# Eight feed-forward tiles that take x1·A2 and nine shift columns, with the second root applied to their sums

## Chip, cores and metric

One core of a Trainium2 chip runs the program. The metric is the device time of one execution in microseconds (us), a median over runs. A profiled execution also has a span, from its first to its last instruction.

## The reference

One layer of a decoder on 320 columns: 256 prompt positions and 8 sequences of 8 sample positions, 2048 features. The part that matters here is where the first sub-layer ends and the feed-forward begins. `m` is the output projection of the mixed heads, `gt1`, `sc2` and `sh2` come from a modulation vector per sequence (one for the prompt, one for each sample).

```python
m = concat(ret_out, sgu_out) @ w_o
x = x + gt1 * rmsnorm(m, g_post_mix)                 # x1
h2 = rmsnorm(x, g_pre_ffn) * (1 + sc2) + sh2
f = square(relu(h2 @ w_ff1)) @ w_ff2                 # 8192 inner features
x = x + gt2 * rmsnorm(f, g_post_ffn)
```

Every matrix product is made in float32 from three products of a reduced form: each operand is split into a high and a low part, and high·high, low·high and high·low are added up.

## The kernel before

Features stand on the 128 partitions, in 16 tiles (KB) of 320 columns (T): TP = 256 prompt columns, then TS = 64 sample columns. A weight piece is one load of 1 MB issued by SP (`load_w`): ScalarE (ACT) casts each half of it into `wh`, VectorE (DVE) subtracts to get `wl`, and a tile of output costs 16 times `mm3`, three TensorE (PE) products each with a weight load. Two raw buffers (NRAW) and three pairs of halves (NHALF) rotate.

Four banks (`acc`) hold running sums. `project` runs a matrix output tile by output tile, one bank each; only the first four tiles of w_o and of w_ff1 are made together, input tile by input tile, in all four banks, from pieces stored for that purpose. `done` evicts a tile: in the feed-forward it is `done_1`, a Relu on ACT out of the bank, a square on GpSimd (POOL) and a `split` into high (ACT) and low (DVE).

Between w_o and the feed-forward lies the residual chain. `mean_rsqrt(sums["m"])` gives the first root `rm`. For each of the 16 tiles DVE makes `gm = gm*rm` and `x1 = x1 + gm`, ACT squares x1, and `mean_four` sums the squares of four tiles on PE in four groups of 32 rows. From these sums comes the second root `r2`: DVE copies them out, PE adds the groups (`thirty`), ACT and DVE take the root. Then `modulate` makes `h2 = x1*A2*r2 + SH2`, split in two, for each tile; A2 and SH2 hold nine columns per tile, the prompt's and eight of the samples. The first product of w_ff1 needs the h2 of tile 0. While the chain runs, PE makes the eight prompt states (`prompt_state`, four instructions each) and products of constants that nobody reads (`keep_warm`, L132).

Modulation columns are made a few at a time from w_ada: four loads of 1 MB (`steps`), 32 PE instructions (`ada_products`), then `ada_finish`: a DVE transpose, four PE products with `sel` and DVE scaling. Two such groups for A2 and SH2 are made around the chain (`late`), further ones (`ada_c`, for G2) beside the first tiles of w_ff1.

The code stands in the order of one engine-neutral program. A scheduler puts it in order per engine, by priorities: `ahead()` raises one, `tc.keep_in_program_order` pins an instruction to its place. Every engine then runs its own list in order, and SP its list of loads.

## Time and profile before

| | us |
|---|---|
| median of 3 runs | 1581.99 (1581.36 to 1582.89) |
| the profiled execution, time | 1581.7 |
| the profiled execution, span | 1579.9 |
| PE busy | 1550.3 (98% of the span) |
| DVE, ACT, POOL busy | 803.7, 578.1, 168.9 |
| mean DMA rate | 205 GB/s |

The share of busy time is high on PE in every part, dummy products among it. What a stretch does is read from the windows and the timeline, in us from the start of the span.

### The profile page before, as it was taken

The page shows a single profiled execution, that of the slowest core. Times are in us where ns is not written, and L with a number is a line of the kernel's source. Part 1 is how long each engine was busy: PE and PEld are TensorE (multiplying, and loading weights), DVE is VectorE, ACT ScalarE, POOL GpSimd, SP SyncE. Part 2 cuts the span into 40 slices and gives each one's busy share as a digit, 9 for nine tenths or more (in the row PEclk, how much of TensorE's full clock was granted, in tenths as well). Part 3 has the DMA queues.
Part 4 walks back from the last instruction along what each step waited for, and adds up shares of the span by engine and source line. Part 5 has one row for each costly group of instructions (what it writes and reads, how often), then busy time and mean ns, then how long its engine had stood idle before and what let it go on. Part 6 is the DMA issues. An engine that isn't in the chain of part 4 may idle for free.

```text
span 1579.9 us, 25805 instructions
## 1 busy us (share of the span) xinstructions
PE 1550.3 (98%) x10900; PEld 1447.1 (92%) x10900; DVE 803.7 (51%) x1319; ACT 578.1 (37%) x843; POOL 168.9 (11%) x176
## 2 busy tenths in 40 slices
PE   8999999999999999999999999999999999999995
PEld 6798898888889997789999999999999999999995
DVE  5776566777744446744433344444444444444555
ACT  5332235234433333433333344322344333443331
POOL 0000000001000120421100112000121000221211
PEclk9999999999999999999999999999999999999998
DMA  8978888665777445784444434434344343443442
GB/s 353 379 307 329 309 327 320 243 247 198 274 271 279 170 153 205 281 311 160 157 147 147 160 136 158 152 142 160 139 155 154 140 160 142 152 158 137 159 146 82
DMA packets 57155, 323.91 MB, mean 205 GB/s; under 512 B 5584, under 2 KB 18128, under 8 KB 22096
## 3 DMA queue, kind: packets, MB, share of 16 engines
q1 hardware_dynamic: 56464, 320.98, 54.3%
q8 instruction: 85, 1.39, 0.3%
q10 hardware_dynamic: 576, 1.29, 0.2%
q14 instruction: 30, 0.25, 0.0%
HBM read 314.65 MB, written 7.60 MB: 204 GB/s over the span
## 4 chain that ended last, share of the span: by engine, by line
PE 95%; DVE 2%; DMA 1%; ACT 1%; issue 0%; POOL 0%; SPq 0%; DVEq 0%; ACTq 0%; POOLq 0%
PE acc L295 28%; PE acc L297 28%; PE acc L296 28%; PE ada L202 5%; DVE f L112 1%; PE pn L546 1%; DMA adaw<-in_w_ada_dram 1%; PE pm L173 1%; DMA x<-in_x_dram 1%; PE acc L132 0%; DVE wl L112 0%; DVE z L112 0%; PE adaT L222 0%; PE gate L440 0%; PE po L524 0%
## 5 line engine op out<-in xcount | busy, mean ns | idle before, releaser
L295 PE MATMUL acc<-hi,wh 128*128 128x320 f32 x3072 | 953.4, 311 | 2.9 <-ACT wh L285 1.5
L296 PE MATMUL acc<-lo,wh 128*128 128x320 f32 x3072 | 951.5, 310 | 0.3 <-DVE lo L112 0.2
L297 PE MATMUL acc<-hi,wl 128*128 128x320 f32 x3072 | 950.0, 310 | 1.1 <-DVE wl L112 1.0
L112 DVE TENSOR_TENSOR wl<-raw,wh 128x1024 fp32r<-128x1024 f32 (+1 forms) x386 | 470.4, 1220 | 485.7 <-ACT wh L285 468.6
L285 ACT CAST wh<-raw 128x1024 fp32r<-128x1024 f32 (+1 forms) x386 | 402.8, 1044 | 744.8 <-PE acc L296 699.6
L295 PEld LDWEIGHTS acc<-hi,wh 128*128 128x128 f32 x3072 | 576.3, 188 | 13.4 <-issue 7.0
L296 PEld LDWEIGHTS acc<-lo,wh 128*128 128x128 f32 x3072 | 576.7, 188 | 7.9 <-issue 6.4
L297 PEld LDWEIGHTS acc<-hi,wl 128*128 128x128 f32 x3072 | 576.2, 188 | 7.3 <-issue 5.0
L112 POOL TENSOR_TENSOR a<-rl 128x320 f32<-128x320 f32 x64 | 87.8, 1371 | 705.2 <-ACT rl L815 682.5
L202 PE MATMUL ada<-adaw,csil 128*32 128x512 f32 (+1 forms) x800 | 88.0, 578 | 0.3 <-DMA adaw<-in_w_ada_dram 0.3
L112 DVE TENSOR_TENSOR z<-z,acc 128x320 f32<-128x320 f32 x120 | 57.2, 484 | 49.4 <-PE acc L297 48.6
L112 POOL TENSOR_TENSOR sq<-sq,sq 128x320 f32<-128x320 f32 x28 | 39.7, 1419 | 275.8 <-ACT sq L751 275.7
L112 DVE TENSOR_TENSOR lo<-a,hi 128x320 fp32r<-128x320 f32 x64 | 31.5, 493 | 71.3 <-ACT hi L304 71.3
L202 PEld LDWEIGHTS ada<-adaw,csil 128*32 128x32 f32 x800 | 23.4, 109 | 47.5 <-issue 45.6
L304 ACT CAST hi<-a 128x320 fp32r<-128x320 f32 x64 | 29.4, 459 | 96.5 <-POOL a L112 96.5
L112 DVE TENSOR_TENSOR f<-f,acc 128x320 f32<-128x320 f32 x48 | 23.4, 488 | 67.7 <-PE acc L297 67.7
L112 POOL TENSOR_TENSOR ve<-vts,cst 128x256 f32<-128x256 f32 x16 | 14.0, 902 | 179.5 <-DVE vts L496 179.1
L218 DVE STREAM_TRANSPOSE part<-ada 128x512 f32<-128x512 f32 (+1 forms) x25 | 17.3, 691 | 26.8 <-PE ada L202 26.7
L815 ACT ACTIVATE rl<-acc 128x320 f32<-128x320 f32 x64 | 27.5, 430 | 1.2 <-PE acc L297 1.2
L112 POOL TENSOR_TENSOR mt<-mt,A 128x64 f32<-128x64 f32 x20 | 8.7, 436 | 177.4 <-DVE A L232 176.1
L317 ACT ACTIVATE hi<-mt,SH 128x256 fp32r<-128x256 f32 x32 | 16.3, 509 | 25.1 <-DVE mt L311 20.7
L320 DVE SCALAR_TENSOR_TENSOR lo<-mt,SH,hi 128x256 fp32r<-128x256 f32 x32 | 15.8, 493 | 3.3 <-ACT hi L317 3.3
(165 smaller groups left out, 569.9 us busy)
## 6 DMA issues: line engine op xcount, KB each, us to landing
raw<-in_w_ff_dram SPq DMA_DIRECT2D x128, 1024.0 KB, 4.8
adaw<-in_w_ada_dram SPq DMA_DIRECT2D x96, 1024.0 KB, 7.9
raw<-in_w_in_dram SPq DMA_DIRECT2D x33, 1024.0 KB, 6.0
raw<-in_w_o_dram SPq DMA_DIRECT2D x16, 1024.0 KB, 4.8
raw<-in_w_in_dram SPq DMA_DIRECT2D x13, 960.0 KB, 4.9
s<-in_s_dram SPq DMA_DIRECT2D x8, 512.0 KB, 5.7
out_ss_dram<-s SPq DMA_DIRECT2D x8, 512.0 KB, 3.7
x<-in_x_dram SPq DMA_DIRECT2D x4, 640.0 KB, 6.7
```

The lines of the kernel that those rows point to most:

```text
L112: return (eng or V).tensor_tensor(out=out, in0=a, in1=b, op=op)
L173: PE.matmul(pm[32 * j : 32 * j + 32, :T], ones[:, :32], q[j], start=first, stop=last, tile_position=(0, 32 * j))
L202: mm = PE.matmul(acc[32 * j : 32 * j + 32, :ncol], csil[:, kb, :], ws[kb // nk][:, kb % nk * ncol : (kb % nk + 1) * ncol], start=i < 4, st ...
L218: V.transpose(part[:, :ncol], acc[:, :ncol])
L285: S.copy(wh[:, :n], r)
L295: PE.matmul(acc[:, :T], wh, ah, start=start, stop=False)
L296: PE.matmul(acc[:, :T], wh, al, start=False, stop=False)
L297: PE.matmul(acc[:, :T], wl, ah, start=False, stop=stop)
L304: S.copy(hi, src)
L317: S.activation(hi[:, :TP], t[:, :TP], AF.Identity, bias=Sm[:, f, 0:1])
L320: V.scalar_tensor_tensor(out=lo[:, :TP], in0=t[:, :TP], scalar=Sm[:, f, 0:1], in1=hb[:, :TP], op0=ALU.add, op1=ALU.subtract)
L815: S.activation(rl, acc[:, :T], AF.Relu)
```

## The change

Eight of the 64 tiles of w_ff1 no longer take h2. Since r2 is one number per column, and SH2 one vector per sequence, `W·h2 = r2 * (W·(x1*A2)) + W·SH2`. So a tile's input becomes `hs`: x1*A2, 256 + 64 columns, and behind them the nine columns of SH2 and a zero, 330 columns in all (TX), split into `hx` and `lx`.

- Tiles 0 to 3 are made inside the residual chain, two input tiles per pass p. For each pair DVE makes gm and x1 (`residual`), ACT the high part of the prompt columns (`high`), POOL copies the shift columns and DVE makes the sample columns (`samples`), ACT casts them (`high_s`), DVE makes both low parts (`low`) and ACT squares (`square`). Weight halves are prepared in the same passes (`half_w`, its low part last). `mean_four` follows behind the products. `keep_warm` is gone; four prompt states stand ahead of the chain and four in it, the latter in banks of another pool.
- At the end the four sums are copied to slots (`evict_1`), and r2 is made while the next tiles run. `done_1` multiplies a copied sum by r2 (DVE), adds the shift to the sample columns (DVE), and takes the Relu with the prompt's shift as bias (ACT).
- Tiles 4 to 7 are again four together, and still take `hs`. Tiles 8 to 11 are four together on the true h2, which `extra` makes, two input tiles beside each piece of tiles 4 to 7 and four beside the first pieces of tiles 8 to 11.
- Slots grow from 320 to 330 columns, and NSLOT goes from 89 to 87. The host stores the pieces of tiles 4 to 11 in the four-together form.

```diff
--- before.py
+++ after.py
-NSLOT = 89
+NSLOT = 87
...
-    def mean_four(pm, q, first, last):
+    def mean_four(pm, q, first, last, pin=None):
 
         for j in range(4):
-            PE.matmul(pm[32 * j : 32 * j + 32, :T], ones[:, :32], q[j], start=first, stop=last, tile_position=(0, 32 * j))
+            mm = PE.matmul(pm[32 * j : 32 * j + 32, :T], ones[:, :32], q[j], start=first, stop=last, tile_position=(0, 32 * j))
+            if pin and j == 0:
+                pin(mm)
...
+    def ada_drain(feats, acc):
+
+        ncol = P * len(feats)
+        part = wp.tile([P, 512], F32, tag="part", bufs=1, name=nm("part"))
+        V.transpose(part[:, :ncol], acc[:, :ncol])
+        return feats, part
+
     def ada_finish(feats, acc):
+        ada_scale(*ada_sums(*ada_drain(feats, acc)))
+
+    def ada_sums(feats, part):
 
         nf = len(feats)
         ncol = P * nf
-        part = wp.tile([P, 512], F32, tag="part", name=nm("part"))
-        V.transpose(part[:, :ncol], acc[:, :ncol])
         pv = part[:, :ncol].rearrange("p (i q r) -> p i q r", i=nf, q=4)
         pt = small("adaT")
         for q in range(4):
             PE.matmul(pt[32 * q : 32 * q + 32, : 9 * nf], sel, pv[:, :, q, 0:9], start=True, stop=True, tile_position=(0, 32 * q))
+        return feats, pt
+
+    def ada_scale(feats, pt):
...
+    def half_w(w, c0, pin=None, nb=8, behind=None):
+
+        n = P * nb
+        wh = wp.tile([P, 1024], F32R, tag="wh", bufs=NHALF, name=nm("wh"))
+        wl = wp.tile([P, 1024], F32R, tag="wl", bufs=NHALF, name=nm("wl"))
+        r = w[:, P * c0 : P * c0 + n]
+        ins = S.copy(wh[:, :n], r)
+
+        def low_part():
+            ins = tt(wl[:, :n], r, wh[:, :n].bitcast(F32), ALU.subtract)
+            if pin:
+                pin(ins)
+
+        blocks = [(wh[:, i : i + P], wl[:, i : i + P]) for i in range(0, n, P)]
+        if pin:
+            pin(ins)
+            return blocks, low_part
+        with tc.issue_after(behind) if behind is not None else nullcontext():
+            low_part()
...
+        n = ah.shape[1]
+        PE.matmul(acc[:, :n], wh, ah, start=start, stop=False)
+        PE.matmul(acc[:, :n], wh, al, start=False, stop=False)
+        PE.matmul(acc[:, :n], wl, ah, start=False, stop=stop)
...
-    def prompt_state():
+    def prompt_state(bank):
         h, kt, vt = later.pop(0)
-        pp = new_acc()
+        pp = bank()
...
+    TX = T + 10
+    def evict_1(acc):
+        u = slot("u", F32, (P, TX))
+        S.copy(u, acc[:, :TX])
+        return u
...
+    for _ in range(4):
+        prompt_state(new_acc)
...
+    pin = tc.keep_in_program_order
     pm1 = small("pm")
-    for q in range(4):
+    acc_1 = [new_acc() for _ in range(4)]
+    raws = [load_raw(A["w_ff1"][i]) for i in range(2)]
+    w_1 = [half_w(raws[0], 0), half_w(raws[0], 8), half_w(raws[1], 0)]
+    hs = [None] * KB
+    t4 = [None] * 4
+    dve = [None]
+
+    def residual(fs):
+        for f in fs:
+            pin(tt(gm[f], gm[f], rm, ALU.mult))
+        for f in fs:
+            pin(tt(x1[f], x1[f], gm[f], ALU.add))
+
+    def samples(f, n):
+
+        q, j = f // 4, f % 4
+        if t4[q] is None:
+            t4[q] = slot("ts")[:, : 4 * (TX - TP)].rearrange("p (i c) -> p i c", i=4)
+            G.memset(t4[q][:, :, TS:], 0.0)
+        G.tensor_copy(t4[q][:, j : j + n, TS : TS + 9], SH2[:, f : f + n, :])
+        pin(tt(t4[q][:, j : j + n, :TS].rearrange("p i (b s) -> p i b s", b=NB),
+               xs[q][:, j : j + n, TP:].rearrange("p i (b s) -> p i b s", b=NB),
+               A2[:, f : f + n, 1:9].unsqueeze(3).broadcast_to([P, n, NB, NS]), ALU.mult))
+
+    def high(f):
+        hs[f] = slot("hx", F32R, (P, TX)), slot("lx", F32R, (P, TX))
+        pin(S.activation(hs[f][0][:, :TP], x1[f][:, :TP], AF.Copy, scale=A2[:, f, 0:1]))
+
+    def high_s(f):
+        pin(S.copy(hs[f][0][:, TP:], t4[f // 4][:, f % 4, :]))
+
+    def low(f):
+        hb = hs[f][0].bitcast(F32)
+        lo = hs[f][1]
+        pin(V.scalar_tensor_tensor(out=lo[:, :TP], in0=x1[f][:, :TP], scalar=A2[:, f, 0:1], in1=hb[:, :TP], op0=ALU.mult, op1=ALU.subtract))
+        dve[0] = pin(tt(lo[:, TP:], t4[f // 4][:, f % 4, :], hb[:, TP:], ALU.subtract))
+
+    def square(f):
+        pin(S.activation(gm[f], x1[f], AF.Square))
+
+    def products(k):
+        for i in range(4):
+            mm3(acc_1[i], w_1[k // 2][4 * (k % 2) + i], hs[k], k == 0, k == KB - 1)
+        if k % 4 == 0 and k > 0:
+            mean_four(pm1, gm[k - 4 : k], k == 4, False, pin)
+
+    with ahead():
+        for f in range(2):
+            residual([f])
+            high(f)
+            samples(f, 1)
+            high_s(f)
+        low(0)
+        square(0)
+        square(1)
+    products(0)
+    for p in range(1, 9):
+        f = 2 * p
+        low_part = None
         with ahead():
-            for f in range(4 * q, 4 * q + 4):
-                tt(gm[f], gm[f], rm, ALU.mult)
-                tt(x1[f], x1[f], gm[f], ALU.add)
-                S.activation(gm[f], x1[f], AF.Square)
-            mean_four(pm1, gm[4 * q : 4 * q + 4], q == 0, q == 3)
-        if q < 3:
-            for _ in range(3 if q < 2 else 2):
-                prompt_state()
-            keep_warm(8, new_acc())
+            if p == 1:
+                low(1)
+            if p < 8:
+                residual([f, f + 1])
+                high(f)
+                high(f + 1)
+            if 2 <= p < 7:
+                i = p + 1
+                if i % 2 == 0:
+                    raws.append(load_raw(A["w_ff1"][i // 2]))
+                blocks, low_part = half_w(raws[i // 2], 8 * (i % 2), pin)
+                w_1.append(blocks)
+            if p > 1:
+                low(f - 2)
+            if p < 8:
+                samples(f, 2)
+                high_s(f)
+                high_s(f + 1)
+            if p > 1:
+                low(f - 1)
+            if low_part:
+                low_part()
+            if p < 8:
+                square(f)
+                square(f + 1)
+        if p > 1:
+            products(f - 2)
+        products(f - 1)
+        if p == 3:
+            late.append(ada_b.products(small("ada")))
+        with ahead(), tc.issue_after(dve[0].ins):
+            if p in (2, 5):
+                late[0] = ada_sums(*ada_drain(*late[0]))
+            if p in (3, 6):
+                ada_scale(*late.pop(0))
+        if p in (1, 2):
+            for _ in range(2):
+                prompt_state(lambda: small("pp"))
+    mean_four(pm1, gm[12:], False, True, pin)
+    us = [evict_1(acc) for acc in acc_1]
...
-    w0 = load_w(A["w_ff1"][0])
-    late.append(ada_b.products(small("ada")))
-    h2 = []
-    for f in range(KB):
-        with ahead() if f < 3 else nullcontext():
-            h2.append(modulate(x1[f], r2, A2, SH2, f, V if f < 3 else G))
-        if f in (6, 9):
-            ada_finish(*late.pop(0))
...
+            if c == 0 and m < 8:
+                u = us[m] if m < 4 else evict_1(acc)
+                tt(u[:, :T], u[:, :T], r2, ALU.mult)
+                tt(sam(u), sam(u), u[:, T + 1 : T + 9].unsqueeze(2).broadcast_to([P, NB, NS]), ALU.add)
+                S.activation(rl[:, :TP], u[:, :TP], AF.Relu, bias=u[:, T : T + 1])
+                S.activation(rl[:, TP:], u[:, TP:T], AF.Relu)
+            else:
+                S.activation(rl, acc[:, :T], AF.Relu)
             tt(a, rl, rl, ALU.mult, G)
             act[m] = split(a)
 
-        project("w_ff1", 16 * c, KB, h2, nat, c == 0, lambda: steps(ada_c, 1) if c == 0 else None, done_1, w0 if c == 0 else None)
+        if c == 0:
+            steps(ada_c, 4)
+            for i in range(4):
+                done_1(i, acc_1[i])
+            h2 = []
+
+            def extra(n):
+                steps(ada_c, 1)
+                for f in range(len(h2), min(len(h2) + n, KB)):
+                    h2.append(modulate(x1[f], r2, A2, SH2, f))
+
+            project("w_ff1", 0, 8, hs, nat, (4,), lambda: extra(2), done_1, 4)
+            project("w_ff1", 0, KB, h2, nat, (8,), lambda: extra(4), done_1, 8)
+        else:
+            project("w_ff1", 16 * c, KB, h2, nat, (), lambda: None, done_1)
```

Place 1, the chain on PE and DVE. In the names, `ada` are modulation products, `pm` the sums of squares, `hx` and `lx` high and low of `hs`. On PE before, from the first square on:

```order
L173 MATMUL pm_6394<-gm_5443,ones 32x320 [waits PE_49,Activation_49]
L173 MATMUL pm_6394<-gm_5451,ones 32x320 [waits Activation_49]
L132 MATMUL acc_6429<-ones,thirty 128x128 [waits DVE_49]
L132 MATMUL acc_6429<-ones,thirty 128x128 x4
L173 MATMUL pm_6394<-gm_5457,ones 32x320 [waits Activation_49]
L132 MATMUL acc_6429<-ones,thirty 128x128
L173 MATMUL pm_6394<-gm_5463,ones 32x320 [waits Activation_49]
L132 MATMUL acc_6429<-ones,thirty 128x128 x2
```

The products of an input tile now stand in that place; here the input tile 6 and the start of the next:

```order
L325 MATMUL acc_6419<-lx_6589,wh_6525 128x330 [waits DVE_49]
L326 MATMUL acc_6419<-hx_6588,wl_6526 128x330
L325 MATMUL acc_6420<-lx_6589,wh_6525 128x330
L204 MATMUL ada_6638<-adaw_6416,csil 32x512 [waits DMAHW5_49]
...
L204 MATMUL ada_6638<-adaw_6410,csil 32x512 x4
L326 MATMUL acc_6420<-hx_6588,wl_6526 128x330
...
L324 MATMUL acc_6419<-hx_6591,wh_6525 128x330 [waits Activation_49]
L325 MATMUL acc_6419<-lx_6592,wh_6525 128x330 [waits DVE_49]
```

Squares and dummies alternated before; now the second modulation group stands inside input tile 6, and the sums of squares come four in a row elsewhere. On DVE before, one pair of tiles and the start of the next:

```order
L112 TENSOR_TENSOR gm_5694<-gm_5694,r_6362 128x320
L112 TENSOR_TENSOR gm_5761<-gm_5761,r_6362 128x320
L112 TENSOR_TENSOR xs_5561<-xs_5561,gm_5694 128x320 [waits DVE_49]
L112 TENSOR_TENSOR xs_5561<-xs_5561,gm_5761 128x320 [waits DVE_49]
L112 TENSOR_TENSOR gm_5856<-gm_5856,r_6362 128x320
L112 TENSOR_TENSOR gm_5925<-gm_5925,r_6362 128x320
```

and with the change, from one weight half to the next:

```order
L112 TENSOR_TENSOR wl_6597<-raw_6594,wh_6596 128x1024 [waits DMAHW4_49,PE_49,Activation_49]
...
L112 TENSOR_TENSOR xs_5859<-xs_5859,gm_5856 128x320 [waits DVE_49]
L112 TENSOR_TENSOR xs_5859<-xs_5859,gm_5925 128x320 [waits DVE_49]
L856 SCALAR_TENSOR_TENSOR lx_6589<-xs_5561,A_119,hx_6588 128x256
L112 TENSOR_TENSOR lx_6589<-ts_6530,hx_6588 128x74 [waits Activation_49]
L112 TENSOR_TENSOR ts_6674<-xs_5859,A_119 128x2x64 [waits DVE_49]
L856 SCALAR_TENSOR_TENSOR lx_6592<-xs_5561,A_119,hx_6591 128x256
L112 TENSOR_TENSOR lx_6592<-ts_6530,hx_6591 128x74 [waits Activation_49]
L112 TENSOR_TENSOR wl_6670<-raw_6594,wh_6669 128x1024 [waits PE_49,Activation_49]
```

The residual of tiles 8 and 9 stands ahead of the low parts of tiles 6 and 7, and a weight's low part stands between.

Place 2, ACT where a group of four tiles ends (`rl` the Relu, `a` its square made by POOL, `u` the copied sum). Before, at the end of tiles 0 to 3:

```order
L815 ACTIVATE rl_7004<-acc_6770 128x320 [waits PE_49]
L304 CAST hi_7008<-a_7005 128x320 [waits Pool_49]
L285 CAST wh_7135<-raw_7133 128x1024 [waits DMAHW2_49,PE_49,Activation_49]
L815 ACTIVATE rl_7012<-acc_6771 128x320
L304 CAST hi_7016<-a_7013 128x320 [waits Pool_49]
L815 ACTIVATE rl_7020<-acc_6772 128x320
L304 CAST hi_7024<-a_7021 128x320 [waits Pool_49]
```

With the change, at the end of tiles 4 to 7:

```order
L810 COPY u_7337<-acc_6975 128x330 [waits PE_49]
L938 ACTIVATE rl_7335<-u_7337 128x256 [waits DVE_49]
L939 ACTIVATE rl_7335<-u_7337 128x64 [waits DVE_49]
L300 CAST wh_7525<-raw_7523 128x1024 [waits DMAHW2_49,PE_49]
L333 CAST hi_7344<-a_7336 128x320 [waits Pool_49]
L810 COPY u_7350<-acc_6976 128x330
L938 ACTIVATE rl_7348<-u_7350 128x256 [waits DVE_49]
L939 ACTIVATE rl_7348<-u_7350 128x64 [waits DVE_49]
L333 CAST hi_7357<-a_7349 128x320 [waits Pool_49]
L810 COPY u_7363<-acc_6977 128x330
```

A bank's copy now stands behind the Relu and the high part of the bank before it, as a bank's Relu did before. What follows on PE is another: before, tile 4 alone in one bank; now tiles 8 to 11, which take all four banks.

Place 3, the loads on SP. Before, after the last pieces issued in w_o, the four loads of the second modulation group stood in a row:

```order
L278 DMA raw_6884<-in_w_ff_dram 128x2048 [waits DMAHW2_49,DVE_49]
L264 DMA adaw_6386<-in_w_ada_dram 128x2048 [waits PE_49]
L264 DMA adaw_6388<-in_w_ada_dram 128x2048 [waits PE_49]
L264 DMA adaw_6390<-in_w_ada_dram 128x2048 [waits PE_49]
L264 DMA adaw_6392<-in_w_ada_dram 128x2048 [waits PE_49]
```

With the change, a weight piece stands ahead of the last of them:

```order
L594 DMA out_sp_dram<-stp_6390 128x128 [waits Activation_49]
L278 DMA adaw_6412<-in_w_ada_dram 128x2048 [waits PE_49]
L278 DMA adaw_6414<-in_w_ada_dram 128x2048 [waits DMAHW3_49,PE_49]
L291 DMA raw_6719<-in_w_ff_dram 128x2048 [waits DMAHW4_49,DVE_49]
L278 DMA adaw_6416<-in_w_ada_dram 128x2048 [waits DMAHW5_49,PE_49]
```

The load of `raw_6719` takes the buffer that a DVE subtraction inside the chain sets free.


## Rows read from the trace of the kernel before

**Rows 1.** The chain that ended last, share of the span by engine:
```profile
PE 95%; DVE 2%; DMA 1%; ACT 1%; issue 0%; POOL 0%; SPq 0%; DVEq 0%; ACTq 0%; POOLq 0%
```

**Rows 2.** Windows; start:end, length, then busy time (instructions) by engine, clock, DMA:
```profile
614.00:626.00 12.00, 12.00 (x81) 6.77 (x74) 11.75 (x30) 4.50 (x15) 0.00 (x0) 1.00 0.94 364
626.00:636.00 10.00, 9.24 (x58) 5.40 (x56) 3.87 (x9) 3.46 (x11) 0.00 (x0) 1.00 0.14 41
636.00:642.00 6.00, 5.13 (x48) 2.07 (x47) 4.58 (x14) 1.79 (x4) 2.74 (x8) 1.00 0.55 206
642.00:675.00 33.00, 32.94 (x240) 29.13 (x240) 26.99 (x66) 17.24 (x39) 14.44 (x32) 1.00 0.81 320
...
1570.00:1580.00 10.00, 0.00 (x0) 0.00 (x0) 5.69 (x7) 0.00 (x0) 0.00 (x0) 0.50 0.60 234
```

**Rows 3.** Timeline of PE: start, length, instruction, count, idle time before it:
```profile
611.19 0.70 PE L180 MATMUL pm<-sq,ones 128*128 128x320 f32 x2
...
616.27 1.60 PE L562 MATMUL acc<-vt,kt 128*128 128x128 f32 x12
...
634.06 0.75 PE L173 MATMUL pm<-gm,ones 128*32 128x320 f32 x8
635.56 0.81 PE L186 MATMUL pm<-pm,thirty 128*128 128x320 f32 x2 [0.76 <-DVE pm L185]
636.30 3.64 PE L202 MATMUL ada<-adaw,csil 128*32 128x512 f32 x32
639.75 0.25 PE L222 MATMUL adaT<-part,cst 128*32 128x36 f32 x8
640.65 0.85 PE L295 MATMUL acc<-hi,wh 128*128 128x320 f32 x4 [0.65 <-ACT hi L318]
...
669.72 0.31 PE L295 MATMUL acc<-hi,wh 128*128 128x320 f32 x1
...
673.97 0.31 PE L297 MATMUL acc<-hi,wl 128*128 128x320 f32 x1
```

**Rows 4.** PE by line, 614 to 642 (L132) and 640 to 674.1 (L295):
```profile
L132 PE MATMUL acc<-ones,thirty 128*128 128x128 f32 x48 | 7.5, 290 | 0.0
...
L295 PE MATMUL acc<-hi,wh 128*128 128x320 f32 x64 | 19.1, 310 | 0.6 <-ACT hi L318 0.6
```

**Rows 5.** Timeline of DVE, 614 to 650:
```profile
615.27 0.49 DVE L168 SCALAR_TENSOR_TENSOR r<-rq,rq 128x320 f32<-128x320 f32 x1
615.80 0.89 DVE L112 TENSOR_TENSOR gm<-gm,r 128x320 f32<-128x320 f32 x2
...
628.67 0.70 DVE L218 STREAM_TRANSPOSE part<-ada 128x512 f32<-128x512 f32 x1
...
640.25 0.47 DVE L320 SCALAR_TENSOR_TENSOR lo<-mt,SH,hi 128x256 fp32r<-128x256 f32 x1
...
641.93 0.21 DVE L112 TENSOR_TENSOR mt<-mt,SH 128x64 f32<-128x64 f32 x1
...
648.86 1.21 DVE L112 TENSOR_TENSOR wl<-raw,wh 128x1024 fp32r<-128x1024 f32 x1
```

**Rows 6.** Timelines of ACT and POOL, 645 and 673 to 678:
```profile
645.51 1.04 ACT L285 CAST wh<-raw 128x1024 fp32r<-128x1024 f32 x1
...
673.00 0.44 ACT L815 ACTIVATE rl<-acc 128x320 f32<-128x320 f32 x1 [1.25 <-PE acc L297]
674.26 0.46 ACT L304 CAST hi<-a 128x320 fp32r<-128x320 f32 x1 [0.83 <-POOL a L112]
...
673.51 0.72 POOL L112 TENSOR_TENSOR a<-rl 128x320 f32<-128x320 f32 x1 [16.19 <-ACT rl L815]
676.08 1.66 POOL L112 TENSOR_TENSOR a<-rl 128x320 f32<-128x320 f32 x1 [1.85 <-ACT rl L815]
```

**Rows 7.** The modulation loads, all 96, from issue to landing:
```profile
DMA to landing us min/median/max: 4.7/7.9/16.4
```

More of the change, by code (lines that the diff above doesn't have):

```diff
@@ L272, in steps, with load_raw, load_w @@
         it.steps(n)
-    def load_w(src, ncol=KB, eng=None, behind=None):
+    def load_raw(src, ncol=KB):
         w = wp.tile([P, 2048], F32, tag="raw", bufs=NRAW, name=nm("raw"))
         nc.sync.dma_start(w[:, : P * ncol], src)
-        blocks = []
-        for c0 in range(0, ncol, 8):
-            n = P * min(8, ncol - c0)
-            wh = wp.tile([P, 1024], F32R, tag="wh", bufs=NHALF, name=nm("wh"))
-            wl = wp.tile([P, 1024], F32R, tag="wl", bufs=NHALF, name=nm("wl"))
-            r = w[:, P * c0 : P * c0 + n]
-            S.copy(wh[:, :n], r)
-            with tc.issue_after(behind) if behind is not None else nullcontext():
-                tt(wl[:, :n], r, wh[:, :n].bitcast(F32), ALU.subtract, eng)
-            for i in range(0, n, P):
-                blocks.append((wh[:, i : i + P], wl[:, i : i + P]))
-        return blocks
+        return w
+    def half_w(w, c0, pin=None, nb=8, behind=None):
[14 more added lines that the diff above has]
+            low_part()
+        return blocks
+    def load_w(src, ncol=KB, behind=None):
+        w = load_raw(src, ncol)
+        return sum([half_w(w, c0, nb=min(8, ncol - c0), behind=behind) for c0 in range(0, ncol, 8)], [])
     def mm3(acc, w, a, start, stop):
@@ L917, in _layout, with full @@
     r["w_in"] = f(np.concatenate(out, 0))
[L919 removed]
+    def full(w, order, fours):
         k, n = w.shape
@@ L922, in full @@
         out = w4.transpose(2, 1, 0, 3).reshape(n // P, P, 2048).copy()
[L923 removed]
+        for m in fours:
             for pc in range(4):
                 ks = order[4 * pc : 4 * pc + 4]
[L926 removed]
+                out[m + pc] = w4[ks][:, :, m : m + 4, :].transpose(1, 0, 2, 3).reshape(P, 2048)
         return out
     nat = list(range(KB))
[L930 to L931 removed]
+    r["w_o"] = f(full(g["w_o"][0], list(range(8, 16)) + list(range(8)), (0,)))
+    r["w_ff1"] = f(full(g["w_ff1"][0], nat, (0, 4, 8)))
     w2 = g["w_ff2"][0]
[L933 removed]
+    r["w_ff2"] = f(np.concatenate([full(w2[D * c : D * (c + 1)], nat, ()) for c in range(NC_FF)], 0))
     return r
```

25 lines of the change are left out of this document (7 added, 18 removed).

## The prediction

> **What bounds the kernel now.** I looked first at the chain that ended last: PE holds 95% of it [rows 1], so an engine beside PE counts only where it keeps PE from useful work. The windows show where that is. From 642 on PE is busy all the time (32.94 of 33 us), at a granted clock of 1.00, its upper level of 2.4 GHz. Between 614 and 642 it looks nearly as busy (26.4 of 28 us) [rows 2]. The timeline of PE shows what it does there: w_o ends at 611.19 and the first product of w_ff1 starts at 640.65 [rows 3], 29.5 us later. In between DVE is the busy engine (11.75 of the first 12 us), and 48 of PE's instructions are dummies of L132, 7.5 us of records [rows 2, 4]. So the stretch is a chain on DVE and ACT with PE kept occupied, and here alone PE has time to give.
>
> **Work that stays.** From 640.65 to the end of the span are 939.25 us. The first group of four tiles ends at 674.1 (its last product starts at 673.97). It holds 64 products on each of three lines, 192; two product starts that lie 29 products apart, 669.72 and 673.97, make 0.1466 us each, 28.15. With one modulation group of 3.6 and one small product set of 0.25 that is 32.0 of 33.45 us, so 1.45 are bubbles of the old start [rows 3, 4]. PE's work from the first product on is 937.8 us, and I take it as unchanged.
>
> **The new start.** The first root is written at 615.76, as now [rows 5]: the work ahead of it keeps its order on ACT and DVE. PE has, behind w_o, two root sums of 0.70 each, four prompt states of four instructions at 0.13 (2.1), and one modulation group of 3.6: 611.19 + 7.1 = 618.3 [rows 3]. The first tile's high part needs gm, x1 and one ACT instruction, about 617.6, and its low part one more of DVE. So PE starts at 618.3, not at 640.65.
>
> **What comes onto PE's path** because nothing hides it any more [rows 3]:
> - The second modulation group, 3.6, and its small set, 0.25. Before they stood in the gap.
> - Four prompt states in the chain, 16 × 0.13 = 2.1.
> - Four sums of squares. Four squares ready together took 0.75, so 3.0.
> - The product that joins the groups, 0.81. It moves from an idle stretch into tiles 4 to 7.
> - Ten more columns in 2 × 192 products. No row shows a product of 330 columns. Bounds are nothing, if the columns are not what sets 0.1466, and 10/320 of it, 4.6 ns. I take the upper, 1.75 us, since each column must pass.
>
> Together 11.5 us. The dummies fall away at no gain of their own: they stood in waiting time.
>
> **Can DVE keep up?** A pair of tiles costs it four instructions of 0.44, two low parts of 0.47 + 0.21 and the sample columns, 0.21: 3.3 us; with a weight half (1.21) 4.5 us [rows 5]. PE needs 24 × 0.151 = 3.6 for the pair. DVE is the slower one only in the five passes that prepare weights. All its work in the chain (32 × 0.44, 16 × 0.68, 9 × 0.21, five halves, two transposes of 0.70, eight small instructions) is 36 us, so it ends near 652. PE's own list in the chain is 29.05 for 192 products, two modulation groups (the first G2 group is placed in input tile 12), 7.2, states 2.1, three sums 2.25, two small sets 0.5: 41.1, so it ends near 659.5, plus bubbles. PE remains the bound, but with little lead early on, where I walked through the orders instruction by instruction:
> - input tiles 0 and 2 wait some 0.1 each for a low part;
> - input tile 6 waits 0.8: its low part stands on DVE behind a weight half, which waits for the ACT cast (1.04), which stands behind two high parts [rows 6];
> - inside input tile 7 the small product set waits 0.75 for the DVE transpose of the modulation group that ended only just before;
> - from there PE is behind DVE.
>
> That is 1.75 us of bubbles. The chain then ends with its last sum of squares at about 662.0 instead of 674.1. The four copies and r2 lie beside tiles 4 to 7, whose first banks are free when needed: the copies start while later banks still add. If that cover were gone, the copies would cost 0.44 each.
>
> **The border between tiles 7 and 8.** Four tiles follow four tiles, and all banks are wanted at once. On ACT a bank's copy stands behind the previous bank's Relu and high part, which wait for DVE's scaling and POOL's square. One link is copy 0.44, scaling 0.49 + 0.21, Relu 0.44 and more for its sample part, square 0.72, high part 0.46, some 3.0 us [rows 5, 6]. The last bank is free three links after the first copy, near 9.0 us behind the end of tile 7 (a weight subtraction stands between on DVE). PE's list puts a modulation group (3.6), a small set and 27 products of the other banks ahead of it: 7.8 us. So 1.2 us of waiting; bounds are none, and 4.0 if every square takes 1.66 as in the second row of POOL.
>
> **Sum.** 618.3 + 937.8 + 11.5 + 1.75 + 1.2 = 1570.55 us of span against 1579.9, 9.35 us less. The profiled execution took 1581.7, 1.8 more than its span, and the median of the runs is 0.3 above that: 1572.35 by the profile, **1572.6** as a median. The other work moved costs nothing: the modulation of h2 (16 times three POOL instructions and four each of DVE and ACT) lies beside tiles 4 to 11, 56 us of PE time, where PE alone is busy throughout; if it came late, tile 8 would wait for it.
>
> **Rivals.**
> - *The relay at the border is longer.* POOL's square took 0.72 in one row and 1.66 in the next, beside a DVE subtraction [rows 6]. Three slow ones add 2.8: 1575.4. For it: DVE has weight halves and scalings at that place. Against it: at the end of tiles 0 to 3, where these rows stand, one was slow and the one before it not. The Trainium skill, "SBUF — State Buffer", Who interferes with whom, says more: a DVE instruction with two SBUF inputs excludes a reading GpSimd instruction for its whole length. By that rule a square could wait out a whole subtraction of 1.21 each time, three times, and the time would be 1576.2; the slow row agrees in kind with its 0.94 more. Chance 0.13.
> - *DVE and ACT set the pace through the chain.* Each weight half waits for PE to free a buffer, ACT to cast, DVE to subtract, and the next residual stands behind it. If all 16 input tiles waited 0.3, 4.8 us would go where I count 1.75: 1575.7. Chance 0.12.
> - *Loads come late.* The fourth load of the second modulation group is issued behind a weight piece that waits for a DVE subtraction, near 626.3, and PE stands at that group in input tile 6 near 634.2 (six input tiles of 1.81, the states, one sum, one small set and a part of tile 6 behind the start). The usual landing of 7.9 us fits just so; the longest, 16.4, makes PE wait 8.5: 1581.1 [rows 7]. For it: the rate was 364 GB/s where four such loads ran together. Against it: here two run [rows 2]. Chance 0.08, mostly below 1578.
> - *Slower: the clock falls.* The dummies go, and PE has bubbles in the chain. After its last work PE is granted 0.50, the lower level of 1.2 GHz [rows 2]. Work at that level takes twice as long; of the 41 us of PE work in the chain, 9.4 would have to run there to use up the gain, and all of it would give 1614. Against it: 636 to 642, with PE busy only 5.13 of 6 us, was granted 1.00, and the expected bubbles are below 1 us each. The Trainium skill, "TensorE: Matmul & The Clock Gate", What's actually happening, calls the throttled state the default that activity lifts, so that rule speaks for the dummies; at idle stretches as long as those of this chain's rows the trace does not show a fall. Chance 0.05.
> - *It doesn't do what it says*: gained time comes back as a wait nobody has listed, as slots of 330 columns that are not free. Then within 0.2%, 1579 to 1585. Chance 0.05.
>
> **How the numbers follow.** The forecast, 1569.5 to 1575, has 0.57. The low end without any bubble and without column cost is 1572.6 − 2.95 − 1.75 = 1567.9, with little chance; I set 1569.0. The upper end takes in the relay, the pace and the milder loads: 1578.5. What a measurement can tell from no change is about 0.2%, 3.2 us: faster is below 1578.8. Forecast, relay and pace lie there whole, and most of the loads: 0.86. Within 0.2%: 0.08, from late loads and the unlisted wait. Slower: 0.06, the clock and what else adds to it.
>
> **What the profile will show.** First product of 330 columns near 618; 192 of them by about 662, with two modulation groups among them; bubbles at input tiles 6 and 7; product starts 0.151 apart; no dummies; a short wait of PE for ACT before the third and fourth bank of tiles 8 to 11; clock 1.00. Wrong would be: product starts no more than 0.147 apart, PE waiting for DVE in most input tiles, a modulation group that waits for its load, or a granted clock below 1.00 between 614 and 700.

## The result, and the profile after

Four runs of the changed kernel have a median of 1572.88 us (1572.06 to 1574.06), four of the kernel before 1582.44 (1581.36 to 1583.09). The ratio is 0.9940, with a 95% interval of 0.9928 to 0.9951: 9.6 us faster, where 1572.6 was predicted. The profiled execution took 1572.06, with a span of 1570.1.

The page of the changed kernel, its busy times and the chain that ended last by engine:

```profile
PE 1540.7 (98%) x10852; PEld 1441.7 (92%) x10852; DVE 817.9 (52%) x1367; ACT 591.3 (38%) x891; POOL 174.3 (11%) x198
...
PE 90%; issue 4%; DVE 2%; POOL 1%; DMA 1%; ACT 1%; SPq 0%; DVEq 0%; POOLq 0%; ACTq 0%
```

PE's share of the span is 98% as before, and its busy time is 9.6 us shorter. Most of that lies in the chain, as its windows show (columns as in [rows 2]: start:end and length, then PE, PE's weight loads, DVE, ACT and POOL, then granted clock, DMA share and GB/s):

```profile
614.00:626.00 12.00, 12.00 (x95) 9.37 (x92) 11.30 (x29) 7.55 (x22) 0.00 (x0) 1.00 0.76 284
626.00:636.00 10.00, 8.39 (x62) 6.31 (x65) 9.15 (x26) 6.21 (x16) 0.33 (x1) 1.00 0.68 240
636.00:642.00 6.00, 6.00 (x56) 3.72 (x49) 4.63 (x13) 1.15 (x3) 0.00 (x0) 1.00 0.79 296
642.00:662.00 20.00, 20.00 (x143) 15.40 (x142) 11.42 (x27) 10.11 (x23) 0.80 (x1) 1.00 0.83 335
```

PE is busy for all but 1.61 us of the 48, against 26.4 of 28 us in [rows 2], and at the upper clock, 1.00, throughout. DMA no longer falls to 0.14 between 626 and 636: a weight piece of tiles 0 to 3 (issued at 625.72) and the last load of the second modulation group (626.45) come in there. The timeline of PE names the pieces that the prediction spoke of:

```profile
610.53 0.70 PE L182 MATMUL pm<-sq,ones 128*128 128x320 f32 x2
...
617.55 0.88 PE L324 MATMUL acc<-hx,wh 128*128 128x330 f32 x4
...
629.32 0.75 PE L173 MATMUL pm<-gm,ones 128*32 128x320 f32 x8
...
633.30 0.42 PE L325 MATMUL acc<-lx,wh 128*128 128x330 f32 x1 [0.62 <-DVE lx L112]
...
635.01 3.64 PE L204 MATMUL ada<-adaw,csil 128*32 128x512 f32 x32 [0.98 <-DMA adaw<-in_w_ada_dram]
...
662.00 0.74 PE L173 MATMUL pm<-gm,ones 128*32 128x320 f32 x8
...
663.69 0.70 PE L188 MATMUL pm<-pm,thirty 128*128 128x320 f32 x2
...
702.47 0.41 PE L324 MATMUL acc<-hi,wh 128*128 128x320 f32 x1 [0.17 <-ACT u L810]
705.38 0.41 PE L324 MATMUL acc<-hi,wh 128*128 128x320 f32 x1 [0.16 <-ACT u L810]
```

Work on w_ff1 starts 7.0 us behind the first root sum, where it started 29.5 behind it [rows 3]. The last sum of squares starts at 662.00. Four waits of PE are left, 0.62, 0.98, 0.17 and 0.16 us.

The first root sum (the row of 610.53; 611.19 in [rows 3]) comes 610.05 to 612.91 us into the span, and differs by 1.5 us between two profiles of the changed kernel itself (610.53 and 612.07). For a difference of one or two us I therefore compare below, beside the timed ratios, **the rest**: a profiled span less the start of that row. It is 1579.9 − 611.19 = 968.7 us before, 1570.1 − 610.53 = 959.6 after, 959.3 in a second profile of the changed kernel.

The rest has a grain of its own. The last 5500 products of w_ff1 and w_ff2 and what follows them are work that no edit touches. They take 827.0 us in the kernel before and its three variants below, 826.25 in both profiles of the changed kernel, and 825.8 to 826.4 in its variants. So 0.8 of the 9.6 us lie there, in products that start 146.5 ns apart instead of 146.7 on the mean; no run shows why. And between the changed kernel and a variant of it, half a us of the rest says nothing of the stretch that was edited.

### The profile page after: what moved, and what is told of

The parts are those of the page before. It is cut to its first block, busy times and chain, and to the rows that moved or that the text cites. A ratio compares the mean times of both kernels' runs of the same rounds, so it can differ in the third digit from the quotient of the medians.

```text
span 1570.1 us, 25814 instructions
## 1 busy us (share of the span) xinstructions
PE 1540.7 (98%) x10852; PEld 1441.7 (92%) x10852; DVE 817.9 (52%) x1367; ACT 591.3 (38%) x891; POOL 174.3 (11%) x198
## 4 chain that ended last, share of the span: by engine, by line
PE 90%; issue 4%; DVE 2%; POOL 1%; DMA 1%; ACT 1%; SPq 0%; DVEq 0%; POOLq 0%; ACTq 0%
PE acc L324 27%; PE acc L326 27%; PE acc L325 27%; PE ada L204 5%; POOL mt L112 1%; DVE f L112 1%; PE pn L575 1%; DMA adaw<-in_w_ada_dram 1%; DMA x<-in_x_dram 1%; DVE wl L112 0%; POOL a L112 0%; DVE z L112 0%; PE gate L469 0%; PE po L553 0%; PE adaT L232 0%
## 5 line engine op out<-in xcount | busy, mean ns | idle before, releaser
L324 PE MATMUL acc<-hi,wh 128*128 128x320 f32 x2944 | 913.1, 310 | 2.6 <-ACT wh L300 1.5
L326 PE MATMUL acc<-hi,wl 128*128 128x320 f32 x2944 | 910.6, 310 | 1.1 <-DVE wl L112 1.0
L325 PE MATMUL acc<-lo,wh 128*128 128x320 f32 x2944 | 910.7, 310 | 0.0
L324 PEld LDWEIGHTS acc<-hi,wh 128*128 128x128 f32 x2944 | 553.1, 188 | 13.5 <-issue 7.0
L326 PEld LDWEIGHTS acc<-hi,wl 128*128 128x128 f32 x2944 | 553.0, 188 | 8.9 <-issue 6.7
L325 PEld LDWEIGHTS acc<-lo,wh 128*128 128x128 f32 x2944 | 553.0, 188 | 4.3 <-issue 3.9
L325 PE MATMUL acc<-lx,wh 128*128 128x330 f32 x128 | 40.5, 317 | 0.6 <-DVE lx L112 0.6
L326 PE MATMUL acc<-hx,wl 128*128 128x330 f32 x128 | 40.6, 318 | 0.0
L324 PE MATMUL acc<-hx,wh 128*128 128x330 f32 x128 | 39.1, 320 | 0.0
L326 PEld LDWEIGHTS acc<-hx,wl 128*128 128x128 f32 x128 | 24.2, 189 | 2.6 <-issue 2.5
```

Source lines behind the costliest of these rows:

```text
L324: PE.matmul(acc[:, :n], wh, ah, start=start, stop=False)
L325: PE.matmul(acc[:, :n], wh, al, start=False, stop=False)
L326: PE.matmul(acc[:, :n], wl, ah, start=False, stop=stop)
```

## The experiments

A quoted passage is what was expected of a run before it was made. The column "before" is the median of the kernel before, timed beside the run on the same chip.

| run | median, us | before | ratio (95%) | rest, us |
|---|---|---|---|---|
| e1_no_dummies | 1579.04 | 1582.94 | 0.9978 (0.9969 to 0.9987) | 964.5 |
| e2_four_tiles | 1582.34 | 1582.94 | 0.9995 (0.9986 to 1.0004) | 968.3 |
| e3_320_columns | 1571.34 | 1582.94 | 0.9923 (0.9911 to 0.9936) | 956.7 |
| e4_ada_later | 1572.10 | 1582.94 | 0.9930 (0.9918 to 0.9943) | 958.3 |
| after_again | 1573.45 | 1583.26 | 0.9947 (0.9933 to 0.9961) | 959.3 |
| e8_both | 1571.86 | 1583.26 | 0.9928 (0.9915 to 0.9941) | 957.7 |
| e6_dve_more | 1573.27 | 1583.26 | 0.9941 (0.9928 to 0.9954) | 959.8 |
| e7_pe_more | 1575.41 | 1583.26 | 0.9959 (0.9946 to 0.9972) | 962.5 |
| e9_four_tiles_busy | 1585.81 | 1583.06 | 1.0018 (1.0010 to 1.0027) | 971.5 |
| e10_states_first | 1583.15 | 1583.06 | 1.0006 (0.9996 to 1.0015) | 969.7 |
| e11_sums_together | 1578.07 | 1582.64 | 0.9971 (0.9960 to 0.9983) | 963.9 |

### The dummies alone

The kernel before, without the dummies of the chain:

```diff
             for _ in range(3 if q < 2 else 2):
                 prompt_state()
-            keep_warm(8, new_acc())
```

> The kernel before, with the 24 dummy products of the residual chain taken out and nothing else. Theory (the chain on DVE and ACT sets the old start, PE has time to give): no change, 1580.5 to 1584, first product of w_ff1 again some 29 us behind the end of w_o, granted clock 1.00 in that stretch. Rival 1 (the dummies themselves cost PE time, and their removal is a good part of the gain): 3 to 6 us faster. Rival 2 (the dummies hold the clock up): granted clock below 1.00 around the first products of w_ff1, and some us slower.

It was faster, by 3.5 us of the ratio and 4.2 by the rest: the theory of no change fell. So this part of the change has a gain of its own, which the prediction denied. The granted clock stayed at 1.00 between 606 and 640 although PE had waits there; the dummies held up nothing that these rows show. The kernel's PE timeline, from the last sums on:

```profile
628.56 1.13 PE L173 MATMUL pm<-gm,ones 128*32 128x320 f32 x4 [0.47 <-ACT gm L789]
630.37 0.73 PE L173 MATMUL pm<-gm,ones 128*32 128x320 f32 x2 [0.68 <-ACT gm L789]
631.74 0.81 PE L186 MATMUL pm<-pm,thirty 128*128 128x320 f32 x2 [0.65 <-DVE pm L185]
```

Now PE waits for squares (1.9 us over 16 sums), and the joining product comes 20.1 us behind the root sum at 611.65; before it came 24.4 behind [rows 3]. My first explanation was the order on ACT: copies of prompt states, which stood behind dummies on PE, stand ahead of squares there. The next run tests it: the dummies stay, and the eight states go ahead of the chain.

```diff
+    for _ in range(8):
+        prompt_state()
     pm1 = small("pm")
...
-            for _ in range(3 if q < 2 else 2):
-                prompt_state()
             keep_warm(8, new_acc())
```

> The kernel before with its dummies kept, and the eight prompt states placed ahead of the chain instead of among the dummies. Theory (the dummies cost time only because prompt states stood behind them on PE, and ACT's copies of these states stood ahead of squares): as fast as the kernel before without dummies, a gain of 3 to 4 us with all 24 dummies still there, and the last square ends 0.5 us behind the last x1. Rival (the dummies delay the sums of squares on PE itself): no gain, 1 us at most.

No gain: 1.0006. ACT did as the theory had it, and the time stayed. The last square on ACT, the copy of the sums on DVE, and PE's last sum:

```profile
630.69 0.47 ACT L791 ACTIVATE gm<-xs 128x320 f32<-128x320 f32 x1 [0.93 <-DVE xs L112]
```

```profile
637.34 0.49 DVE L185 COPY pm<-pm 128x320 f32<-128x320 f32 x1 [6.68 <-PE pm L173]
```

```profile
635.64 0.94 PE L132 MATMUL acc<-ones,thirty 128*128 128x128 f32 x6
636.51 0.73 PE L173 MATMUL pm<-gm,ones 128*32 128x320 f32 x2
```

The squares are done at 631.2, and the last sum starts 5.3 us later, without a wait on PE. So PE's own list was late, and ACT's order was not the cause. That sent me back to the kernel before. Its PE rows between 616.27 and 634.81 name no wait at all; three of them, and all sums and states by line:

```profile
620.20 0.72 PE L173 MATMUL pm<-gm,ones 128*32 128x320 f32 x2
620.85 0.49 PE L132 MATMUL acc<-ones,thirty 128*128 128x128 f32 x2
621.27 0.73 PE L173 MATMUL pm<-gm,ones 128*32 128x320 f32 x2
```

```profile
L173 PE MATMUL pm<-gm,ones 128*32 128x320 f32 x32 | 8.3, 445 | 0.0
...
L562 PE MATMUL acc<-vt,kt 128*128 128x128 f32 x32 | 4.7, 285 | 0.0
```

One sum alone (two records) takes 0.65 us from its start to the next row's; four in a row took 0.75 [rows 3]. In the code each of the four takes another 32 columns of the array (`tile_position`), and by these times four of them run side by side. Counted from start to start, the 18.5 us hold 7.6 of sums, 6.7 of dummies and 4.2 of states. If that list sets the length of the chain, putting the sums four in a row must help as much as taking the dummies out, with all dummies kept:

```diff
-            mean_four(pm1, gm[4 * q : 4 * q + 4], q == 0, q == 3)
+        if q > 0:
+            mean_four(pm1, gm[4 * q - 4 : 4 * q], q == 1, False)
         if q < 3:
...
             keep_warm(8, new_acc())
+    mean_four(pm1, gm[12:], False, True)
```

(`mean_four` pins each product to its place, so that the four stay together.)

> The kernel before with all 24 dummies and all prompt states in their places; only the 16 sums of squares are made four in a row, one quarter later than their squares (the last two quarters behind the dummies). Theory, formed after the last runs (PE's own list of 18.5 us without a wait, from 616.27 to 634.81, sets the length of the chain before; its largest part are sums that stand alone at 0.65 us each, where four in a row take 0.67): PE then ends its list some 5 us earlier, DVE's last x1 near 629.4 sets the end, and the kernel is 3 to 4.3 us faster than before, as it was without dummies. Rival (what the dummies cost is ACT's order, where copies of states stand ahead of squares): 1 us at most, since that order stays.

It was faster by 4.6 us (0.9971; 4.8 by the rest), with the 24 dummies in place:

```profile
620.66 0.80 PE L173 MATMUL pm<-gm,ones 128*32 128x320 f32 x8
...
628.27 1.27 PE L173 MATMUL pm<-gm,ones 128*32 128x320 f32 x12
629.99 1.13 PE L173 MATMUL pm<-gm,ones 128*32 128x320 f32 x4 [0.45 <-ACT gm L789]
631.77 0.81 PE L186 MATMUL pm<-pm,thirty 128*128 128x320 f32 x2 [0.65 <-DVE pm L185]
```

The joining product comes 19.5 us behind the root sum at 612.27, and the wait in front of the last sums is one for squares. So in the kernel before PE set the chain's pace, and DVE and ACT follow some 5 us behind as the next bound.

About half of the 9.6 us of the change can thus be had without any algebra, by the order of the sums alone. Against this kernel the changed one is shorter by 4.3 to 4.6 us of the rest (963.9 to 959.6 and 959.3), the 0.8 us of untouched products among them.

### Four tiles or eight

Here tiles 4 to 7 take the true h2, which `modulate` makes for the first four input tiles ahead of the Relus of tiles 0 to 3:

```diff
-            if c == 0 and m < 8:
-                u = us[m] if m < 4 else evict_1(acc)
+            if c == 0 and m < 4:
+                u = us[m]
...
-            project("w_ff1", 0, 8, hs, nat, (4,), lambda: extra(2), done_1, 4)
-            project("w_ff1", 0, KB, h2, nat, (8,), lambda: extra(4), done_1, 8)
+            project("w_ff1", 0, KB, h2, nat, (4, 8), lambda: extra(4), done_1, 4)
```

> The changed kernel, but only tiles 0 to 3 take x1*A2; tiles 4 to 7 take the true h2, as before the change every tile did. Theory (the second four tiles are the cover for the second root and the first h2): PE stands idle some 5 to 6 us behind the last sum of squares, 1.3 us come back because 192 products have 320 columns again: 4 to 5 us slower than the changed kernel, 1576.5 to 1578. Rival (the early start alone is the gain, the root is short): within 1.5 us of the changed kernel, 1571.5 to 1574.5.

The whole gain is gone: 0.9995, and a rest 8.7 us above that of the changed kernel, about twice the loss that was expected. The chain runs as there (last sum at 662.39), and then PE has nothing to do. Its timeline and windows:

```profile
663.80 0.81 PE L188 MATMUL pm<-pm,thirty 128*128 128x320 f32 x2 [0.66 <-DVE pm L187]
...
669.77 1.17 PE L324 MATMUL acc<-hi,wh 128*128 128x320 f32 x3 [4.96 <-ACT hi L347]
...
671.90 0.47 PE L326 MATMUL acc<-hi,wl 128*128 128x320 f32 x1
672.17 0.47 PE L325 MATMUL acc<-lo,wh 128*128 128x320 f32 x1
```

```profile
665.00:670.00 5.00, 0.23 (x1) 0.23 (x2) 4.96 (x19) 1.48 (x5) 2.01 (x3) 0.64 0.99 418
667.00:673.00 6.00, 3.23 (x11) 2.84 (x12) 6.00 (x25) 3.19 (x10) 2.01 (x3) 0.50 0.52 216
670.00:675.00 5.00, 5.00 (x24) 4.21 (x28) 5.00 (x19) 2.75 (x9) 1.02 (x1) 0.68 0.04 13
...
680.00:690.00 10.00, 9.28 (x62) 8.76 (x61) 8.95 (x17) 6.43 (x15) 8.98 (x20) 1.00 0.87 347
```

Waits of 0.66 and 4.96 us stand where the changed kernel has products of tiles 4 to 7. The granted clock falls within the idle time: 0.64 and 0.68 are means over both levels, and from 667 to 673 it is 0.50, the lower one. The products there start 0.27 apart, not 0.147. From 680 to 720 PE idles another 1.7 us by the windows, while h2 is made for the next input tiles. The four further tiles are thus what covers the root and h2; without them this gap returns, and it takes with it what the chain gave.

The next run fills the gap with dummies, to see what the clock's part is:

```diff
         r2 = mean_rsqrt(None, pm1)
+    keep_warm(22)
```

> The kernel with four tiles on x1*A2 again, with 22 dummy products on PE behind the product that joins the sums, 22 x 0.22 = 4.8 us, where PE was idle for 4.96 us and its granted clock then fell to 0.64 and 0.68. Theory (the idle stretch brings the clock down, and the first products pay for it): the clock stays at 1.00, the products behind the gap start 0.147 apart from the first on instead of 0.265, which is worth some 1.2 us against the run with four tiles; the remaining loss against the changed kernel, some 7.5 us, stays, since it is the wait for h2 itself. Rival (the clock is of no account, or the dummies delay the root): the same time as with four tiles, or longer.

The clock's part came as expected, and the time did not: 1.0018, 3.2 us above the run without these dummies by the rest.

```profile
665.71 5.08 PE L132 MATMUL idle<-ones,thirty 128*128 128x128 f32 x44
...
673.34 0.31 PE L324 MATMUL acc<-hi,wh 128*128 128x320 f32 x1
673.49 0.31 PE L325 MATMUL acc<-lo,wh 128*128 128x320 f32 x1
...
684.64 0.85 PE L324 MATMUL acc<-hi,wh 128*128 128x320 f32 x4 [1.88 <-ACT hi L346]
...
685.69 0.47 PE L325 MATMUL acc<-lo,wh 128*128 128x320 f32 x1
685.95 0.47 PE L326 MATMUL acc<-hi,wl 128*128 128x320 f32 x1
```

```profile
665.00:670.00 5.00, 4.94 (x41) 4.78 (x42) 4.57 (x11) 1.07 (x3) 1.68 (x3) 1.00 1.01 421
670.00:675.00 5.00, 4.79 (x39) 4.29 (x39) 5.00 (x22) 2.84 (x9) 0.63 (x1) 1.00 0.29 118
...
680.00:690.00 10.00, 8.12 (x52) 7.41 (x49) 6.70 (x16) 4.49 (x11) 8.06 (x18) 0.83 0.91 381
...
686.00:688.50 2.50, 2.50 (x12) 2.17 (x11) 1.96 (x4) 0.84 (x3) 2.27 (x6) 0.50 1.02 429
```

The clock stays at 1.00 up to 685, products are 0.15 apart from the first on, and PE reaches the fifth input tile before its h2 is there: a wait of 1.88 us. The first products behind it are 0.15 apart too; then the clock falls after all (0.50 from 686 to 688.5), and they are 0.27 apart. PE's idle time between 670 and 720 sums to 4.8 us, against 1.7 in the run without dummies. A PE that is faster in front of late data only waits later. Why the data came later still, I leave open: the scheduler also put a weight half, a modulation group and its scaling elsewhere, so the two kernels differ in more than the dummies.

### What sets the pace inside the new chain

One more DVE multiplication of 320 columns for each input tile, into a tile that nobody reads (one slot fewer makes room for it):

```diff
             pin(tt(x1[f], x1[f], gm[f], ALU.add))
+        for f in fs:
+            pin(tt(spare, gm[f], rm, ALU.mult))
```

> One more DVE multiplication of 320 columns for each of the 16 input tiles of the chain, 16 x 0.41 = 6.5 us, its result unread. Theory (PE sets the pace of the chain, DVE's tight stretch is the passes up to input tile 7): the part of 6.5 us that falls in the tight stretch is paid, some 1.5 to 3 us more than the changed kernel, and DVE's lateness is gone by input tile 10. Rival (DVE sets the pace through the whole chain): 6 us or more, with PE waiting for DVE in most input tiles.

Both missed: 0.9941, as the changed kernel itself (0.9947 beside it; 0.2 to 0.4 us more by the rest, which is within its grain). The waits of PE in this kernel, 609 to 740:

```profile
PE acc L325 <- DVE lx L112: 2.2, 2, 1.9
```

PE does wait for DVE twice in the early input tiles, 2.2 us instead of 0.6. But it comes later to the modulation group, whose load has landed by then: the wait of 0.98 is gone, and so are the two at the border. 6.5 us of work on DVE cost 0.6 us between the root sum and the last sum of squares (52.0 us, 51.5 in the changed kernel), since DVE itself had waited 7.2 us in the chain of the changed kernel, the longest time in this row of its timeline:

```profile
654.96 0.72 DVE L219 STREAM_TRANSPOSE part<-ada 128x512 f32<-128x512 f32 x1 [3.20 <-PE ada L204]
```

Three dummies on PE behind each of eight passes, 24 in all:

```diff
         products(f - 1)
+        keep_warm(3)
```

> Three dummy products behind each of eight passes, 24 in all; in the kernel before 24 such products made 5.3 us at their spacing of 0.22. Theory (PE sets the pace): 3.7 to 5.3 us more than the changed kernel, the early ones absorbed by the waits of 0.6 and 1.0. Rival (DVE or the loads set the pace, PE has slack): 1 us or less.

By the rest 2.9 to 3.2 us more, by the timed runs 1.9 to 2.0, with intervals that overlap. The eight groups take 0.6 to 0.9 us each from start to start, 5.6 in all, and the waits of 0.62 and 0.98 are gone: 4.0 would be left, of which about 1 doesn't show in the rest. Both are less than the 3.7 that the theory gave at the least, and more than the rival's 1 us. With the run before it, this makes PE the one that sets the pace of the new chain, with 1.6 us of slack in the first half: there work for DVE is nearly free and work for PE beyond that slack is not.

### The terms that could be taken back

The second modulation group one pass later (`p == 4` for `p == 3`):

> The changed kernel with the second modulation group's products asked for one pass later (p == 4). In the trace of the changed kernel PE waits 0.98 us in input tile 6 for the group's last load. Theory (loads are a small part, one wait): that wait goes, 0.5 to 1.2 us faster than the changed kernel, 1571.7 to 1572.4. Rival (PE has no lead over DVE here, so another wait takes its place): no change, PE then waits for low parts of input tiles 6 to 9.

The wait for its load is gone and no other came: the rest is 1.0 to 1.3 us shorter. The ratio is 0.9930, with an interval that overlaps the changed kernel's, so the timed runs alone do not show the gain. The same with the four sums of tiles 4 to 7 copied out in a row ahead of their Relus:

```diff
-        if p == 3:
+        if p == 4:
             late.append(ada_b.products(small("ada")))
...
+                if name == "w_ff1" and m == 4:
+                    with ahead():
+                        us.extend(evict_1(acc) for acc in accs)
                 for i in range(4):
                     done(m + i, accs[i])
```

> The second modulation group one pass later, and the four sums of tiles 4 to 7 copied out ahead of any Relu. Theory (both waits stand on PE's path and nothing else takes their place): faster than the changed kernel by 0.98 + 0.65 = 1.6 us, of which the later group gives about 1 as it did alone; PE waits for no load and for no copied sum. Rival (the copies only move the wait: with all four copies ahead, the Relu and the squares of tiles 4 to 7 come later, and PE has them behind the border): gain of the later group alone, 0.8 to 1.0 us.

> The changed kernel once more, as the yardstick of the runs beside it on the same chip. Expected: the ratio to the kernel before stays at 0.994, within 0.0011 either way, and the same two early waits of PE (0.6 us for DVE in input tile 6, 1.0 us for a modulation load) appear in the profile. If the load wait is a matter of the execution and not of the order of loads, it will differ by over 0.5 us here.

All that is left of PE's waits between 609 and 740 in the kernel with both edits is this row:

```profile
PE acc L325 <- DVE lx L112: 0.7, 1, 0.7
```

Its median is 1571.86, the changed kernel's beside it 1573.45; the rest is 1.6 to 1.9 us shorter than in the two profiles of the changed kernel. The two intervals overlap, so the timed runs alone do not prove it; its rows show the waits gone. It is the fastest kernel here that computes the layer in full. The changed kernel's second profile had the same two early waits, 0.63 and 0.77.

Then the ten columns. In this kernel the products of tiles 0 to 7 take 320 columns, and SH2 itself is added where the product of W with it belongs:

```diff
-            mm3(acc_1[i], w_1[k // 2][4 * (k % 2) + i], hs[k], k == 0, k == KB - 1)
+            mm3(acc_1[i], w_1[k // 2][4 * (k % 2) + i], (hs[k][0][:, :T], hs[k][1][:, :T]), k == 0, k == KB - 1)
...
-                tt(sam(u), sam(u), u[:, T + 1 : T + 9].unsqueeze(2).broadcast_to([P, NB, NS]), ALU.add)
+                tt(sam(u), sam(u), smod(SH2, m), ALU.add)
```

> The changed kernel with products of tiles 0 to 7 over 320 columns; the shift columns are still copied and cast, but not multiplied, and SH2 itself is added to the sums in place of its product, so the shift is left out of the computation. This measures the ten columns alone. Theory: 384 products at 0.1466 us instead of 0.151 to 0.154, so 1.7 to 2.6 us faster than the changed kernel, about 1570.7. Rival (columns are not what sets the spacing of products): no change, product starts 0.151 or more apart.

The rest is 2.6 to 2.9 us shorter than that of the changed kernel. Over the products of tiles 0 to 7 that follow one another without a wait or anything else between, the mean spacing of starts is 151.9 ns in the changed kernel and 146.3 here: 5.6 ns for ten columns, 2.1 us for 384 products. Of the remaining 0.5 to 0.8 us, 0.3 lie in the untouched last 5500 products (825.9 for 826.25). What is left I can't place; PE's waits are not it, since they sum to 2.0 us here and 1.9 in the changed kernel.

## Why the prediction held, and where it did not

- **What bounds the kernel now: wrong in one step.** "So the stretch is a chain on DVE and ACT with PE kept occupied" failed. PE's list of 18.5 us without a wait was the bound, and the run with the sums together shows it. For the same reason "the dummies fall away at no gain of their own" is wrong: alone they give some 4 us, and the sums four in a row 4.6. The rows were there: no idle time stood beside any PE row of L132 in [rows 4] or of L562 in [rows 3]. I read the dummies' presence as PE waiting.
- **Why the total held all the same.** The sum counted PE's work in the new kernel one by one, from a start that rests on the first root. What the dummies and the lone sums cost before does not enter it. It did count the sums at 0.75 for four, as they then stood. From the root sum to the end it made 1570.55 − 611.19 = 959.4 us; measured are 959.6 and 959.3. That it came out so close is luck in part: the chain took 1.4 us more than listed, and what follows it some 1.1 less.
- **The new start.** 7.1 us behind the root sum, measured 7.0. Its place in the span, 617.55 for 618.3, follows w_o, which ended 0.66 earlier.
- **The chain's length.** The last sum was to end near 662.0, that is 50.8 us behind the root sum; it started 51.5 behind it, and ended about 0.7 after that. Some 1.4 us more than listed: where a set of sums, a modulation group or a small product set stands between products, the product ahead of it and the one behind it each take 0.1 us longer (655.39 to 655.63 to 656.30 to 656.56 around one set of sums), which the list had left out. Two such places, near 646.4 and 653.9, are part of the 1.45 us that "Work that stays" took off as bubbles of the old start. Behind the chain some 1.1 us come back: 0.3 at the border, below, and 0.8 in the untouched products, which the sum took as unchanged.
- **Bubbles.** 1.75 predicted, 1.60 measured, of other make: 0.62 at input tile 6 (0.8 predicted), nothing at tiles 0 and 2, nothing for the transpose in tile 7. In their place stands 0.98 of the late load, which I had as a rival with up to 8.5, and as a sign of being wrong. Its mechanism is what happened; the later group removes it. That the sum of the bubbles agrees is luck: 0.95 of listed waits did not come, and 0.98 that the sum did not hold did.
- **Ten columns.** 1.75 predicted as the upper bound, 2.1 by the spacing. The bound was too low: it took 10/320 of the spacing, and the increase is 5.6 ns, not 4.6.
- **The border.** 1.2 predicted, 0.33 measured. PE could use the last bank 8.7 us behind the end of tile 7 (from 696.64 to the row of 705.38), where 9.0 was predicted. Its own list ahead of that took 8.4 instead of 7.8, with the same 0.1 us around a group, so less of it was waiting. The four squares on POOL took 0.72 each, as the sum had them, since none met a weight subtraction; the first three:

```profile
697.19 0.72 POOL L112 TENSOR_TENSOR a<-rl 128x320 f32<-128x320 f32 x1 [7.07 <-ACT rl L939]
700.87 0.72 POOL L112 TENSOR_TENSOR a<-rl 128x320 f32<-128x320 f32 x1 [2.97 <-ACT rl L939]
703.78 0.72 POOL L112 TENSOR_TENSOR a<-rl 128x320 f32<-128x320 f32 x1 [2.19 <-ACT rl L939]
```

  and the subtraction that follows the first of them on DVE starts after its end:

```profile
698.08 1.23 DVE L112 TENSOR_TENSOR wl<-raw,wh 128x1024 fp32r<-128x1024 f32 x1
```

  So the rival of slow squares did not come about. The Trainium skill, "SBUF — State Buffer", Who interferes with whom, has a DVE instruction with two inputs in SBUF exclude a reading GpSimd instruction; here no square met one, so the rule was not put to the test at this place. In the run with 22 dummies a square beside the subtraction of 677.12 (1.21 us) took twice as long, which agrees with it in kind:

```profile
677.46 1.44 POOL L112 TENSOR_TENSOR a<-rl 128x320 f32<-128x320 f32 x1 [2.08 <-ACT rl L940]
```

- **DVE and ACT at the pace: no.** DVE's last low part ends at 651.8, as predicted (near 652), and 6.5 us more on DVE cost next to nothing.
- **The clock: no.** It stayed at 1.00 in the whole chain. The run with four tiles shows that the danger is real one step further: without the four further tiles it fell within the idle 4.96 us.

## What to carry to other kernels

An engine that executes filler is not an engine that has time: add up its own list from start to start, and look for a wait beside its rows, before you call the filler free. Small products that use a quarter of the array each cost here as much alone (0.65 us) as four of them together (0.67 to 0.75), so let the order keep them in fours, even if the first ones wait. And work that commutes with a late factor has to be long enough: half of it closed the chain and left the gap behind it, so that nothing was gained.
